# Trunk of two layers on one core: row multiplications on GpSimd, row scalings tied to chunks, operands emitted earlier

## The chip, the cores and the metric

The kernel runs on one core of a Trainium2 chip. A core has five engines with queues of their own: TensorE (PE, matmuls; PEld are its weight loads), VectorE (DVE), ScalarE (ACT), GpSimd (POOL) and SyncE (SP, which here only issues transfers). The metric is the device time of one execution in microseconds, the median of the runs shown.

## The reference

A sequence of 1024 rows and 1024 columns goes through two layers. Each layer is a mixer and a convolutional feed-forward network (FFN), and both end in a residual sum, a layer norm and a gain.

```python
e = jax.nn.silu(c @ cond_w + cond_b)
for i in range(DEPTH):
    mod = (e @ ada_w[i] + ada_b[i])[:, None, :]
    sh1, sc1, g1, sh2, sc2, g2 = jnp.split(mod, 6, axis=-1)
    y = mixers[i % N_MIXERS](x * (1.0 + sc1) + sh1)
    x = layer_norm(DN_ALPHA * x + (1.0 + g1) * y, ln_g[i, 0], ln_b[i, 0])
    y = conv_ffn(x * (1.0 + sc2) + sh2, ffn_up[i], ffn_conv_w[i], ffn_conv_b[i], ffn_down[i])
    x = layer_norm(DN_ALPHA * x + (1.0 + g2) * y, ln_g[i, 1], ln_b[i, 1])
```

The mixer of layer 0 is a gated delta net, that of layer 1 is retention: four heads, chunks of 128 rows, a state carried from chunk to chunk, each row of a head's output standardized and multiplied by a gate, then an output projection. Everything is float32.

## The kernel before

**Products.** Each float32 operand is split in two: ScalarE copies it into the high part (line 89) and VectorE subtracts that from the operand to make the low part (line 90). A product is then three matmuls: high by low, low by high, high by high (lines 110 to 112, 301 to 303, 716, 1585). Large products use schemes with seven block products in place of eight: `strassen` computes the input projections (the FFN's up and gate, retention's q, k and gate), and `proj_gen` the three projections back to 1024 columns, which are layer 0's FFN down, retention's output and layer 1's FFN down.

**The order.** The program emits instructions one after the other and gives them to a planner, which puts them in order on each engine by its own estimates, so an instruction can run well ahead of its place in the program. In the stretches with `pq`, `pm` and `ptr`, TensorE's order is written by hand: `run` walks several streams on a clock of its own (the dictionary `RL` has its delays). A load waits on SP until its buffer is free, and what is queued behind it on SP waits as well.

**The projections.** `proj_gen` runs seven block products. In each it loops over blocks `j`: `ops` loads and splits the pair of operands, twelve matmuls use it, and the next weight block is loaded (`load_b`, line 1451). When a product's sums are complete, `f1` to `f7` take them out. `finish` turns a sum of 128 x 512 into a residual row: it multiplies by the gate row G (line 1506), adds the scaled old row (line 1508) and takes statistics (line 1509). `norm` then needs a power, which runs on GpSimd (line 1516). `finish` runs 16 times in each projection, four times for each pair (half, nh). The pair (1, 0) gets its sum straight from PSUM, the other three from SBUF.

**Retention.** `ret_v` computes the values, half a head at a time, in four steps of two row blocks; its stream fills TensorE. `core` runs head by head through eight chunks, `ret_front` makes scores, `ret_back` finishes a chunk: statistics (line 1947), a power on GpSimd (line 1951), the normalized rows `on` (line 1953), their transposes on TensorE (line 719), the gate (loaded in line 1957, multiplied in line 1962), and the stores. Chunks 4 to 7 also load two blocks stored by chunk n - 4 (line 1980) and form four sums of blocks on GpSimd (line 1984). At the end of the last value product `ret_fill` starts the output projection, whose blocks fill TensorE beside head 3.

**Background work.** `bg` is a list of small units, one taken at each `bg_step`. For retention, `bg_gain` (lines 405 to 413) puts 16 units there, each of which loads 128 x 512 of the normalized rows, multiplies and adds the layer norm's gain and shift on GpSimd and stores the result `xg` for the residual of the output projection. `bg_ada` puts 8 units there that make the row G on VectorE (line 239). Their buffers have the tag "lane" (four, one held by the decay mask, two by the state) and "xT".

Of the kernel before, what the change touches and what calls it, by code (L numbers as in the profile page):

```python
# [12 lines left out]
ALU = mybir.AluOpType  # L13
# [20 lines left out]
def trunk_kernel(ctx: ExitStack, tc, A):  # L34
# [59 lines left out]
    def after(key):  # L94
        return tc.issue_after(anchor[key].ins) if key in anchor else nullcontext()
# [1177 lines left out]
    def c_of(q, a, b):  # L1273
# [2 lines left out]
        dve.tensor_tensor(b, a, b, ALU.add)  # L1276
        return b

    def strassen(hT0, xts, scale, shift, items, tags=("hTb", "hTb", "qkv", "qkv", "aux"), direct=False, late=()):
        B = {"11": hT0[:4], "21": hT0[4:]}  # L1280
        nblk = [0]
# [7 lines left out]
        def side(n, s):  # L1289
            out = []  # L1290
            for u in items[n][:2]:
                w = held.pop(u.offset, None) or load_w(u)
                if n == 0 and s == 0:
                    held[u.offset] = w
                X = acc_tile()
                for i, b in enumerate((("11", "21"), ("12", "22"))[s]):
                    for k in range(4):
                        mm3(X, w, k + 4 * i, B[b][k], i == 0 and k == 0, i == 1 and k == 3)
                out.append(X)
            return out  # L1300
# [121 lines left out]
    def proj_gen(nj, ablk, wsrc, slots, xsrc, G, final, ln_next, tag, ltags, dst, key, mm=pe.matmul, gate=None):  # L1422
# [80 lines left out]
            return x[nh] if isinstance(x, tuple) else x[:, hs(nh)]  # L1503

        def finish(half, t, nh, c):
            dve.tensor_tensor(c, c, G[nh], ALU.mult)
            xv = xh(half, t, nh)
            dve.scalar_tensor_tensor(xv, xv, ALPHA, c, ALU.mult, ALU.add)
            dve.bn_stats(stats[half][t][:, nh], xv)
# [82 lines left out]
        for st in steps[:ahead]:  # L1592
            load_b(*st)
        hooks = []
        for p, (an, bn, fin, side, fresh) in enumerate(prods):
            if gate and p < 2 or banks[side] is None:
                banks[side] = acc4() if gate and p < 2 or side == 0 else [sc_tile(), sc_tile(), mm_tile(), mm_tile()]
                if gate and p == 1:
                    banks[0] = banks[1]
                    banks[1] = None  # L1600
            accs = banks[0] if gate and p == 1 else banks[side]
            tail = []
            depth = ltags[3] if p == 6 else 2
            for j in range(nj):
                if gate and p < 2:
                    yield gate(j)
                    yield from take("qkv", 2)
                    give("qkv", 2)
                a, w = ops(an, bn, j, not gate and p < (7 if final else 5))
                with after("a"):  # L1610
                    for st in steps[p * nj + j + ahead:p * nj + j + ahead + 1]:
                        load_b(*st)
                if not gate and p == 2 and j % 2 == 0 and j < 8:
                    xload(0, j // 2)
                if final and p == 3 and j % 2 == 0 and j < 8:
                    xload(1, j // 2)
                if p == 2 and j < 4 and gate:
                    xload(0, j)
                    finish(0, j, 0, c11[j])
                if j >= nj - depth:  # L1620
                    tail.append((j, a, w))
                else:
                    for t in range(4):
                        mma(accs[t], t, a, w, fresh and j == 0, False, mm if p < 2 else pe.matmul if fresh else mm_on)
                        yield 0.0
                for _ in range(-(-20 // (nj - 1)) if p == 6 else 4 if p == 5 else 2):
                    if later:
                        later.pop(0)()
                if p == 5 and j > 1 and not later:
                    for _ in range(-(-16 // (nj - 2))):  # L1630
                        if hooks:
                            hooks.pop(0)()
                bg_step()
            while later:
                later.pop(0)()
            if p == 5:
                while hooks:
                    hooks.pop(0)()
            if p == 6:
                pin[0] = None  # L1640
            for t in range(4):
                for j, a, w in tail:
                    mma(accs[t], t, a, w, fresh and j == 0, j == nj - 1, mm if p < 2 else pm_on if p == 6 else pe.matmul if fresh else mm_on)
                fin(t, accs[t])
                yield 0.0
            if p == 1:
                yield "P2"
            if p == 4:
                hooks = [] if final else ln_hooks(0, xts[0], tag, ln_next, outs, dst, key, bal["h"])
                if not final:  # L1650
                    hooks += [lambda t=t: xload(1, t) for t in range(4)]
# [12 lines left out]
    def layer_tail(i, mix, wout, xsrc, x_mid, x_out, ln_next, final):  # L1664
        sc2, sh2 = fold(i, 1, 2 * i)
        if i == 0:
            bg_tag[0] = "xT"
            hT0 = []
            get = out_hl(mix)
            G1 = rows[0, 2]  # L1670
            xts = proj_ln(0, GH, get, wout, xsrc, G1, ("x", i), then=[lambda: bg_ada(0, 5, "row")])
            hooks = ln_hooks(0, xts, "hTa", lambda: (sc2, sh2), hT0, x_mid, ("mid", i), BAL["gh"])
            xts = proj_ln(1, GH, get, wout, xsrc, G1, ("x", i), hooks=hooks)
            hooks = ln_hooks(1, xts, "hTa", lambda: (sc2, sh2), [], x_mid, ("mid", i))
            for h in hooks[KT:]:
                h()
            bg_tag[0] = "wr"
        else:
            mix.append((sc2, sh2))
            hT0, xts = proj_st(mix[0])  # L1680
        bg_gain(2 * i, x_mid, xg[i + 1], "xT")
        if i == 0:
# [78 lines left out]
        while rowq or rowp:  # L1761
            row_step()
        slots = {"c": "hTa", "x": "qkv"}
        gb2 = gain_rows(3, ("mid", i), "hTb") if final else None
        return proj_st(proj_gen(NF // 2, ablk_of(ad, "qkv"), A["ffn_down"][i], slots, xg[i + 1], rows[i, 5],
                       (gb2, x_out) if final else None, ln_next, "hTb", ("hTb", "hTa", 8, 6, "f") if final else ("qkv", "hTa", 8, 4, "0"), x_out, ("out", i)))
# [91 lines left out]
    def ret_v(h, half):  # L1858
        accs = acc4()
        for kp in range(4):  # L1860
            wh, wl = load_w(A["ret_wv"][h, kp])
            for kk in range(2):
                kt = kp * 2 + kk
                hl = hT[half][kt]
                ns = slice(kk * 4, kk * 4 + 4)
                for t in range(4):
                    ts_ = slice(t * P, (t + 1) * P)
                    pm(accs[t], hl[1][:, ts_], wh[:, ns], start=(kt == 0), stop=False)
                    pm(accs[t], hl[0][:, ts_], wl[:, ns], start=False, stop=False)
                    pm(accs[t], hl[0][:, ts_], wh[:, ns], start=False, stop=(kt == KT - 1))  # L1870
                    yield 0.0
            bg_step()
        for t in range(4):
            yield from take("qkv", 2)
            vv = two("qkv", F32R, "vv")
            split(vv[0], vv[1], accs[t])
            va[h].append(vv)
        emit(("rv", h, half), RL["v"])
# [21 lines left out]

    def core(h):
        yield after_ev(("rv", h, 0), ("core", h - 1))
        if h == 2:
            bg_ada(1, 2, "row")
        q, k = load_qk(h, 0), load_qk(h, 1)
        St = None
        yield RL["q"]
        r = ret_front(h, 0, q, k)
# [36 lines left out]
    def ret_back(h, n, po):  # L1945
# [3 lines left out]
        dve.bn_aggr(mv[:, 0:2], st[:, 0])  # L1949
        dve.tensor_scalar(mv[:, 2:3], mv[:, 1:2], 1e-6, None, ALU.add)  # L1950
        pool.tensor_tensor(mv[:, 3:4], mv[:, 2:3], mhalf[:, 0:1], ALU.pow)
        on = tl("t2", [P, HALF], name="on")
        dve.tensor_scalar(on, po, mv[:, 0:1], mv[:, 3:4], ALU.subtract, ALU.mult)
        yield RL["b"]
        sl = slice(n * P, (n + 1) * P)
        g = tl("cv", [P, 516], name="gt")[:, 0:HALF]
# [3 lines left out]
            ptr(pt[:, j * P:(j + 1) * P], on[:, j * P:(j + 1) * P])  # L1960
        ot = tl("cv", [P, 516], name="ot")[:, 0:HALF]
        dve.tensor_mul(ot, pt, g)
        s4 = slice(n % 4 * P, (n % 4 + 1) * P)

        def pair_view(t):
            return t.rearrange("p (j a f) -> p a j f", a=2, f=P)

        def blk(nm):
            return od[2 * h:2 * h + 2, ABLK.index(nm), :, s4].rearrange("j p t -> p j t")

        ov = pair_view(ot)
        if n < 4:
            for a, nm in enumerate(("11", "12")):
# [1 line left out]
            if n == 3:  # L1975
                emit(("ob", h), RL["o"])
            return
        pv = pair_view(tl("cv", [P, 516], name="op")[:, 0:HALF])
        for a, nm in enumerate(("11", "12")):
            sp.dma_start(pv[:, a], blk(nm))  # L1980
        act.dma_start(blk("22"), ov[:, 1])
        for d, x, y, op, nm in ((ov[:, 0], ov[:, 0], ov[:, 1], ALU.add, "S1"), (pv[:, 0], ov[:, 0], pv[:, 0], ALU.subtract, "S2"),
                                (pv[:, 1], pv[:, 1], pv[:, 0], ALU.subtract, "S4"), (ov[:, 1], ov[:, 1], pv[:, 0], ALU.subtract, "S3")):
# [15 lines left out]
    def ret_fill():  # L1999
# [2 lines left out]
                yield from ret_v(h, half)  # L2002
        while bg or pend:
            bg_step()
        slots = {"c": "hTb", "x": "hTb"}
        mix.append(proj_gen(8, ablk_of(od, "qkv"), A["ret_wout"], slots, xg[0], rows[1, 2], None,
                            lambda: mix[1], "hTa", ("qkv", "hTb", 4, 4, "r"), xs[2], ("mid", 1), pm, lambda j: after_ev(("ob", j // 2))))
        for r in mix[0]:
            if r == "P2":
                return  # L2010
            yield r

    mix = []
    bg_gain(1, xs[1], xg[0])
    events["core", -1] = clk[0]
    free["qkv"] = 20
    bg_tag[0] = "xT"
# [105 lines left out]
```

## Time and profile before

| what | value |
|---|---|
| three runs | 2900.12, 2903.78 and 2907.11 us |
| median | 2903.78 us |
| profiled execution | 2897.41 us |
| its span, first to last instruction | 2895.6 us |
| mean granted TensorE clock | 0.989 |
| VectorE busy | 75% of the span |
| GpSimd busy | 17% of the span |

The profile is one execution. Its tables give busy time by engine, the granted clock of TensorE as a share of full speed, and, for a group of instructions or in order of time, what ended the idle time before them. An engine's busy time is the union of its instructions, so a matmul of 390 ns that starts every 226 ns counts 226. Retention with its output projection lies between 1720 and 2240 us, layer 1's FFN follows up to the end, and layer 0's down projection ends at 1391 us.

### The profile page before, as it was taken

How to read it: one execution, taken by the hardware profiler on the slowest of the kernel's cores; microseconds unless marked ns; L12 is line 12 of the kernel's file. 1: busy time of each engine (PE TensorE's matmuls, PEld its weight loads, DVE VectorE, ACT ScalarE, POOL GpSimd, SP SyncE). 2: the span in 40 equal slices, each digit the busy share in tenths (PEclk: the TensorE clock that was granted, in tenths of full speed). 3: DMA queues.
4: the chain of work that ended last, by engine and by line, in shares of the span. 5: the costliest groups of instructions: out<-in, count | busy, mean ns of one | idle time of the engine just before them, and what ended most of it. 6: DMA issues, size and time to landing. Idle time of an engine off the chain costs nothing.

```text
span 2895.6 us, 38913 instructions
## 1 busy us (share of the span) xinstructions
PE 2794.7 (97%) x13594; PEld 2284.7 (79%) x13594; DVE 2184.7 (75%) x3874; ACT 1295.0 (45%) x2387; POOL 490.4 (17%) x509
## 2 busy tenths in 40 slices
PE   8999999999999999999999999999999999999997
PEld 6777887887787878887888877777677788888886
DVE  5787688576788888868677656666689887777779
ACT  4663465344654444545333332222344644444443
POOL 0311221010023232000000022422201023332001
PEclk9998999999999999999999999999999999999999
DMA  7223243164254555845343365655664264434853
GB/s 277 88 95 121 85 139 103 52 240 153 95 189 163 195 181 171 294 153 189 127 146 127 119 233 159 211 165 156 214 217 146 71 196 138 142 132 163 287 182 117
DMA packets 252884, 465.30 MB, mean 161 GB/s; under 512 B 24144, under 2 KB 77776, under 8 KB 252688
## 3 DMA queue, kind: packets, MB, share of 16 engines
q1 hardware_dynamic: 218560, 408.02, 42.9%
q10 hardware_dynamic: 31488, 46.15, 4.3%
q0 software_dynamic: 2640, 8.65, 0.8%
q8 instruction: 107, 1.75, 0.3%
q14 instruction: 89, 0.73, 0.1%
HBM read 346.86 MB, written 115.87 MB: 160 GB/s over the span
## 4 chain that ended last, share of the span: by engine, by line
PE 54%; DVE 23%; DMA 10%; issue 6%; ACT 5%; POOL 1%; SPq 0%; ACTq 0%; DVEq 0%; POOLq 0%
PE acc L716 9%; PE acc L1285 5%; PE acc L1585 4%; PE acc L110 4%; PE acc L111 4%; PE acc L112 4%; PE sc L716 3%; PE sc L1285 3%; DVE o L1719 3%; PE mm L716 2%; DMA mvw<-in_ada_w 2%; DVE wb L90 2%; DMA wr<-in_ffn_up 2%; DVE qkv L490 2%; DVE mm L1339 2%
## 5 line engine op out<-in xcount | busy, mean ns | idle before, releaser
L716 PE MATMUL acc<-hT,wh 128*128 128x512 f32 x960 | 300.0, 394 | 0.0
L1585 PE MATMUL acc<-bb,ab 128*128 128x512 f32 x984 | 230.9, 393 | 6.9 <-DVE ab L90 3.3
L89 ACT ACTIVATE ab<-ar 128x512 fp32r<-128x512 f32 x210 | 131.1, 629 | 220.9 <-PE mm L303 48.3
L1585 PEld LDWEIGHTS acc<-bb,ab 128*128 128x128 f32 x984 | 184.1, 189 | 48.8 <-DVE ab L90 4.1
L716 PEld LDWEIGHTS acc<-hT,wh 128*128 128x128 f32 x960 | 182.8, 190 | 36.0
L90 DVE TENSOR_TENSOR ab<-ar,ab 128x512 fp32r<-128x512 f32 x210 | 149.0, 715 | 81.4 <-ACT ab L89 81.3
L1285 PE MATMUL acc<-T,wb 128*128 128x512 f32 x840 | 202.1, 389 | 0.4 <-DVE wb L90 0.4
L716 PE MATMUL acc<-hT,wl 128*128 128x512 f32 x480 | 197.2, 411 | 3.6 <-ACT sq L509 2.4
L89 ACT ACTIVATE wb<-mm 128x512 fp32r<-128x512 f32 x216 | 124.1, 597 | 167.3 <-DVE mm L1339 158.8
L411 POOL TENSOR_TENSOR xg<-xg,gb 128x512 f32<-128x512 f32 x48 | 66.2, 1380 | 709.5 <-DMA xg<-xs 405.6
L90 DVE TENSOR_TENSOR wl<-wr,wh 128x1024 fp32r<-128x1024 f32 x98 | 123.3, 1258 | 82.8 <-ACT wh L89 82.5
L1285 PEld LDWEIGHTS acc<-T,wb 128*128 128x128 f32 x840 | 157.5, 188 | 34.2 <-ACT o L1720 1.2
L89 ACT ACTIVATE wh<-wr 128x1024 fp32r<-128x1024 f32 x98 | 103.6, 1060 | 148.3 <-PE acc L716 60.1
L90 DVE TENSOR_TENSOR wb<-wr,wb 128x512 fp32r<-128x512 f32 x162 | 114.1, 705 | 64.1 <-ACT wb L89 64.0
L1750 POOL TENSOR_TENSOR o<-o 128x512 f32<-128x512 f32 x80 | 112.5, 1414 | 269.0 <-ACT pc L1355 175.2
L1719 DVE SCALAR_TENSOR_TENSOR o<-g,vc,o 128x512 f32<-128x512 f32 (+2 forms) x176 | 151.3, 870 | 8.1 <-ACT o L1714 6.9
L90 DVE TENSOR_TENSOR wb<-mm,wb 128x512 fp32r<-128x512 f32 x216 | 145.2, 686 | 6.9 <-ACT wb L89 6.9
L1339 DVE TENSOR_TENSOR mm<-wr 128x512 f32<-128x512 f32 x108 | 87.8, 813 | 76.7 <-DMA wr<-in_ffn_up 61.3
L89 ACT ACTIVATE wb<-wr 128x512 fp32r<-128x512 f32 x162 | 101.3, 626 | 94.0 <-PE acc L1285 28.4
L716 PE MATMUL acc<-wh,hT 128*128 128x512 f32 x384 | 135.5, 417 | 1.5 <-DVE vv L90 1.4
L1355 ACT ACTIVATE pc<-acc 128x512 f32<-128x512 f32 x143 | 84.3, 589 | 113.2 <-PE acc L1285 65.0
L239 DVE SCALAR_TENSOR_TENSOR ada<-mvw,e,ada 128x512 f32<-128x512 f32 x140 | 106.9, 763 | 23.7 <-DMA mvw<-in_ada_w 23.4
(672 smaller groups left out, 7420.0 us busy)
## 6 DMA issues: line engine op xcount, KB each, us to landing
wr<-in_ffn_up SPq DMA_DIRECT2D x92, 512.0 KB, 3.9
mvw<-in_ada_w SPq DMA_DIRECT2D x80, 512.0 KB, 4.4
ad<-o SPq DMA_DIRECT2D x154, 256.0 KB, 2.3
ar<-ad SPq DMA_DIRECT2D x154, 256.0 KB, 3.8
Br<-in_ffn_down SPq DMA_DIRECT2D x88, 256.0 KB, 3.5
wr<-in_ret_wv SPq DMA_DIRECT2D x32, 512.0 KB, 4.0
ar<-od SPq DMA_DIRECT2D x56, 256.0 KB, 5.2
wr<-in_gdn_wqkv SPq DMA_DIRECT2D x24, 512.0 KB, 3.6
```

Source lines behind the costliest of these rows:

```text
L89: anchor["sp"] = act.activation(dst_h, src, AF.Copy)
L90: eng.tensor_tensor(dst_l, src, dst_h, ALU.subtract)
L110: mm(acc, wl[:, k], hl[0], start=first, stop=False)
L111: mm(acc, wh[:, k], hl[1], start=False, stop=False)
L112: mm(acc, wh[:, k], hl[0], start=False, stop=last)
L239: dve.scalar_tensor_tensor(a, wr[:, kk], e[:, k:k + 1], a, ALU.mult, ALU.add)
L716: pq(pe.matmul(out, lhsT, rhs, start=start, stop=stop), cost or COST[out.shape[-1]])
L1285: return pe.matmul(*a, skip_group_check=True, **kw)
L1339: dve.tensor_tensor(t, x, y, op)
L1585: return pe.matmul(*args, skip_group_check=True, **kw)
L1719: dve.scalar_tensor_tensor(tv, gv[:, c0 - j:c1 - j], w[:, 2 - j:3 - j], tv, ALU.mult, ALU.add)
L1750: (dve if fp == 0 else pool).tensor_tensor(o[d], o[x], o[y], op)
```

## The change

There are four parts.

1. In `finish` the multiplication by G runs on GpSimd for all but the pair (1, 0).
2. The 16 gain units of retention leave the background list. `ret_back` now calls one `gain_step` right after the power of chunks 0 to 3 of each head, and of chunk 4 of the last head: it finishes the row loaded by the call before and loads the next one. With that list shorter, `ret_v` takes a background step at every other step in heads 0 to 2, and the units of G start at head 1 in place of head 2.
3. The output projection's first pair of operands is loaded and split before the matmuls of the last step of the last value product (`start_out`, which waits until head 3's q and k loads are emitted). In chunks 4 to 7 the two block loads move ahead of the gate load.
4. A projection that is followed by `strassen` loads and splits the first weight of that stage before its last sums (`preload`).

```diff
+    wpre, wnext_up = {}, []
+
+    def preload():
+        while wnext_up:
+            u = wnext_up.pop(0)
+            wpre[u.offset] = load_w(u)
...
-                w = held.pop(u.offset, None) or load_w(u)
+                w = held.pop(u.offset, None) or wpre.pop(u.offset, None) or load_w(u)
...
         def finish(half, t, nh, c):
-            dve.tensor_tensor(c, c, G[nh], ALU.mult)
+            (pool if True and (half, nh) != (1, 0) else dve).tensor_tensor(c, c, G[nh], ALU.mult)
...
+        ready = {}
+        if gate:
+            ready[0, 0] = ops(*prods[0][:2], 0, False)
+            with after("a"):
+                load_b(*steps[ahead])
+            yield "ops"
...
-                a, w = ops(an, bn, j, not gate and p < (7 if final else 5))
-                with after("a"):
-                    for st in steps[p * nj + j + ahead:p * nj + j + ahead + 1]:
-                        load_b(*st)
+                if (p, j) in ready:
+                    a, w = ready.pop((p, j))
+                else:
+                    a, w = ops(an, bn, j, not gate and p < (7 if final else 5))
+                    with after("a"):
+                        for st in steps[p * nj + j + ahead:p * nj + j + ahead + 1]:
+                            load_b(*st)
...
             if p == 6:
                 pin[0] = None
+                preload()
...
             mix.append((sc2, sh2))
+            wnext_up.append(A["ffn_up"][i][1])
...
+        if not final:
+            wnext_up.append(A["ret_wg"][2])
...
             wh, wl = load_w(A["ret_wv"][h, kp])
+            if (h, half, kp) == (RH - 1, 1, 3):
+                yield after_ev(("qk", h))
+                start_out()
...
-            bg_step()
+            if kp % 2 or h == RH - 1:
+                bg_step()
...
-        if h == 2:
+        if h == 1:
             bg_ada(1, 2, "row")
         q, k = load_qk(h, 0), load_qk(h, 1)
+        emit(("qk", h))
...
         pool.tensor_tensor(mv[:, 3:4], mv[:, 2:3], mhalf[:, 0:1], ALU.pow)
+        if n < 4 or h == RH - 1 and n == 4:
+            gains.pop(0)()
         on = tl("t2", [P, HALF], name="on")
         dve.tensor_scalar(on, po, mv[:, 0:1], mv[:, 3:4], ALU.subtract, ALU.mult)
...
+        if n > 3:
+            pv = pair_view(tl("cv", [P, 516], name="op")[:, 0:HALF])
+            for a, nm in enumerate(("11", "12")):
+                sp.dma_start(pv[:, a], blk(nm))
         yield RL["b"]
...
-        pv = pair_view(tl("cv", [P, 516], name="op")[:, 0:HALF])
-        for a, nm in enumerate(("11", "12")):
-            sp.dma_start(pv[:, a], blk(nm))
         act.dma_start(blk("22"), ov[:, 1])
...
-        slots = {"c": "hTb", "x": "hTb"}
-        mix.append(proj_gen(8, ablk_of(od, "qkv"), A["ret_wout"], slots, xg[0], rows[1, 2], None,
-                            lambda: mix[1], "hTa", ("qkv", "hTb", 4, 4, "r"), xs[2], ("mid", 1), pm, lambda j: after_ev(("ob", j // 2))))
         for r in mix[0]:
...
+    def start_out():
+        slots = {"c": "hTb", "x": "hTb"}
+        mix.append(proj_gen(8, ablk_of(od, "qkv"), A["ret_wout"], slots, xg[0], rows[1, 2], None,
+                            lambda: mix[1], "hTa", ("qkv", "hTb", 4, 4, "r"), xs[2], ("mid", 1), pm, lambda j: after_ev(("ob", j // 2))))
+        assert next(mix[0]) == "ops"
...
-    bg_gain(1, xs[1], xg[0])
+    gains, gx = [], []
+
+    def gain_step(m):
+        if gx:
+            x, c, rs, gb = gx.pop()
+            pool.tensor_tensor(x, x, gb[0], ALU.mult)
+            pool.tensor_tensor(x, x, gb[1], ALU.add)
+            sp.dma_start(xg[0][rs, hs(c)], x)
+        if m < 2 * NCH:
+            c, r = divmod(m, NCH)
+            if r == 0:
+                gbs.append([tl("auh", [P, HALF], name="gb") for _ in range(2)])
+                for t, nm in zip(gbs[-1], ("ln_g", "ln_b")):
+                    sp.dma_start(t, A[nm][1:2, hs(c)].to_broadcast([P, HALF]))
+            rs = slice(r * P, r * P + P)
+            x = tl("lane", [P, HALF], name="xg")
+            sp.dma_start(x, xs[1][rs, hs(c)])
+            gx.append((x, c, rs, gbs[-1]))
+
+    gbs = []
+    gains += [lambda m=m: gain_step(m) for m in range(2 * NCH + 1)]
```

More of the change, by code (lines that the diff above doesn't have):

```diff
@@ L1951, in ret_back, with pair_view, blk @@
         pool.tensor_tensor(mv[:, 3:4], mv[:, 2:3], mhalf[:, 0:1], ALU.pow)
+        if n < 4 or h == RH - 1 and n == 4:
+            gains.pop(0)()
         on = tl("t2", [P, HALF], name="on")
         dve.tensor_scalar(on, po, mv[:, 0:1], mv[:, 3:4], ALU.subtract, ALU.mult)
+        s4 = slice(n % 4 * P, (n % 4 + 1) * P)
+        def pair_view(t):
+            return t.rearrange("p (j a f) -> p a j f", a=2, f=P)
+        def blk(nm):
+            return od[2 * h:2 * h + 2, ABLK.index(nm), :, s4].rearrange("j p t -> p j t")
+        if n > 3:
+            pv = pair_view(tl("cv", [P, 516], name="op")[:, 0:HALF])
+            for a, nm in enumerate(("11", "12")):
+                sp.dma_start(pv[:, a], blk(nm))
         yield RL["b"]
@@ L1962, in ret_back @@
         dve.tensor_mul(ot, pt, g)
[L1963 to L1969, printed above, removed]
         ov = pair_view(ot)
```

## The prediction

> **What bounds the kernel now.** I read the page's busy times first, then the busy time in stretches of 20 us, then the engines in order of time around each stretch in which TensorE is not full.
>
> ```profile
> span 2895.6 us, 38913 instructions
> PE 2794.7 (97%) x13594; PEld 2284.7 (79%) x13594; DVE 2184.7 (75%) x3874; ACT 1295.0 (45%) x2387; POOL 490.4 (17%) x509
> ```
>
> TensorE is busy 97% of the span, so 2895.6 - 2794.7 = 101 us of idle TensorE, and what a lowered clock costs, are all that a rearrangement can win anywhere. The change leaves the matmuls alone. It can only shorten waits, and only in the second half, where its places are.
>
> ```profile
> 1320.00:1340.00 20.00, 17.53 (x73) 14.05 (x72) 19.09 (x41) 9.02 (x15) 4.17 (x4) 0.91 0.44 138
> 1360.00:1380.00 20.00, 17.93 (x85) 14.35 (x84) 19.06 (x31) 12.04 (x20) 0.59 (x1) 1.00 0.41 135
> 1720.00:1740.00 20.00, 20.00 (x90) 16.36 (x89) 4.68 (x6) 7.32 (x11) 0.00 (x0) 0.93 0.57 198
> 1820.00:1840.00 20.00, 16.77 (x72) 13.13 (x71) 9.66 (x14) 4.88 (x7) 14.73 (x15) 0.91 0.86 251
> 1900.00:1920.00 20.00, 19.53 (x88) 14.77 (x87) 11.09 (x17) 5.46 (x7) 10.32 (x13) 1.00 0.72 211
> 2180.00:2200.00 20.00, 18.64 (x77) 13.79 (x77) 20.00 (x40) 12.91 (x23) 2.47 (x3) 1.00 0.27 87
> 2200.00:2220.00 20.00, 18.86 (x89) 15.05 (x89) 20.00 (x32) 6.34 (x10) 2.26 (x3) 1.00 0.52 186
> 2860.00:2880.00 20.00, 18.40 (x80) 14.54 (x79) 20.00 (x39) 1.34 (x2) 0.85 (x1) 1.00 0.17 66
> ```
>
> After the stretch and its length come the busy time and count of PE, PEld, DVE, ACT and POOL, then the granted clock. There are two kinds of hole. In the late products of the three projections (1320 to 1380, 2180 to 2220, 2860 to 2880) VectorE is full and TensorE loses 1.1 to 2.5 us a stretch. In retention's first head (1820 to 1840) VectorE is half idle, GpSimd is at 14.73 of 20, and TensorE loses 3.23 us and runs at 0.91.
>
> **Part 1: row scalings behind the powers.** Here is the hole at 1828 in order of time (start, duration, engine, line, operation; in brackets the idle time and its releaser):
>
> ```profile
> 1822.50 0.15 DVE L1950 TENSOR_SCALAR mv<-mv 128x1 f32<-128x1 f32 x1
> 1823.36 1.30 POOL L411 TENSOR_TENSOR xg<-xg,gb 128x512 f32<-128x512 f32 x1 [0.78 <-DMA xg<-xs]
> 1824.73 1.26 POOL L412 TENSOR_TENSOR xg<-xg,gb 128x512 f32<-128x512 f32 x1
> 1825.96 0.72 POOL L1984 TENSOR_TENSOR ot<-ot 128x256 f32<-128x256 f32 x1
> 1826.64 0.55 POOL L1951 TENSOR_TENSOR mv<-mv,mhalf 128x1 f32<-128x1 f32 x1
> 1828.18 0.64 PE L719 MATMUL mm<-cst,on 128*128 128x128 f32 x4 [3.23 <-DVE on L1953]
> ```
>
> The power's input was ready at 1822.65. It started at 1826.64, behind one scaled row (two operations) and a block sum; then VectorE normalized, and TensorE's transposes, whose place in its order is fixed, waited 3.23 us. The same step in head 1, where no scaled row is near:
>
> ```profile
> 1907.32 0.15 DVE L1950 TENSOR_SCALAR mv<-mv 128x1 f32<-128x1 f32 x1
> 1907.97 0.55 POOL L1951 TENSOR_TENSOR mv<-mv,mhalf 128x1 f32<-128x1 f32 x1
> ```
>
> starts 0.50 us after its input. The change puts every scaled row behind the power of one of chunks 0 to 3 (and the last behind head 3's chunk 4); those chunks have no block sums. What should go is 3.23 us of idle and 20 x (1 - 0.91) = 1.8 us of clock, less the 20 - 19.53 = 0.47 us that head 1 still loses in the like stretch: 4.6 us. Bounds: 0, if the power still stands behind something, and 5.0.
>
> The moved work is 16 rows, each with one load, two Pool operations and one store, and four loads of gain and shift rows. Pool's two operations take 2.56 us. Between two powers of early chunks it has room for them:
>
> ```profile
> 1874.32 0.55 POOL L1951 TENSOR_TENSOR mv<-mv,mhalf 128x1 f32<-128x1 f32 x1 [8.45 <-DVE mv L1950]
> ```
>
> 8.45 us idle hide 2.56; without that cover each row would cost up to 2.56 us of the next power. On SP the rows' 36 transfers now stand among the gate and weight loads of all four heads. Today some of them stand somewhere worse, at the end of the stage before:
>
> ```profile
> 1705.97 3.98 SPq L413 DMA_DIRECT2D xg<-xg  x2
> ...
> 1712.41 0.98 SPq L1854 DMA_DIRECT2D xlo<-xs  x2
> ...
> 1718.23 0.44 PE L282 MATMUL mm<-cst,xlo 128*128 128x128 f32 x2 [2.01 <-DMA xlo<-xs]
> ```
>
> SP stood 3.98 us on stores that wait for Pool, with the loads of the lower rows queued behind them, and TensorE waited 2.01 us for those loads. Tied to the chunks, the rows can no longer be drawn forward to this place. I take 2.0 us. Bounds: 0, as these loads also need a free buffer, and 2.0 plus the clock's 20 x (1 - 0.93) = 1.4 us just after, 3.4. The ada rows move from head 2 to head 1 (8 loads, 16 VectorE operations), and half of the background steps go. No TensorE wait of size stands there: 0.
>
> **Part 2: operands split ahead.** The output projection starts with
>
> ```profile
> 2028.71 0.40 PE L716 MATMUL acc<-wh,22_12806 128*128 128x512 f32 x1
> 2029.64 0.62 ACT L89 ACTIVATE ab<-ar 128x512 fp32r<-128x512 f32 x1
> 2031.10 0.68 DVE L90 TENSOR_TENSOR ab<-ar,ab 128x512 fp32r<-128x512 f32 x1
> 2031.84 3.02 PE L716 MATMUL acc<-bb,ab 128*128 128x512 f32 x12 [2.73 <-DVE ab L90]
> ```
>
> TensorE has no filler and waits 2.73 us for the first pair's splits. The change emits this pair (one load and two splits for each of its two operands) before the last quarter of the last value product, so the split is done when that ends. The first pair feeds 12 matmuls, 2.7 us, in which the second pair's splits fit (0.6 us each on ScalarE and VectorE). I take 2.7 us. Bounds: 0, if the wait passes to the second pair, and 2.7. The value product now also waits until head 3's q and k loads are issued; head 3 is in its second chunk by then, so this costs 0. The block loads drawn ahead of the gate load in chunks 4 to 7 help block sums that are not what TensorE waits for after part 1, but they take a buffer earlier: 0, with 2.7 either way, the size of the wait just quoted.
>
> **Part 3: first weights split ahead.**
>
> ```profile
> 1375.43 1.23 DVE L90 TENSOR_TENSOR wl<-wr,wh 128x1024 fp32r<-128x1024 f32 x1
> ...
> 1391.52 0.39 PE L110 MATMUL acc<-hT,wl 128*128 128x512 f32 x1
> ```
>
> ```profile
> 2213.33 1.23 DVE L90 TENSOR_TENSOR wl<-wr,wh 128x1024 fp32r<-128x1024 f32 x1
> ...
> 2223.53 0.48 PE L110 MATMUL acc<-hT,wl 128*128 128x512 f32 x1
> ```
>
> Both first weights are already split 15 and 9 us before their first matmul. Emitting load, copy and split earlier moves nothing that is late: 0. The most it could cost is one split, 1.2 us, ahead of the last sums.
>
> **Part 4: rows multiplied on GpSimd.** Twelve of 16 in each projection move, 36 in all.
>
> ```profile
> 2210.32 2.50 DVE L1506 TENSOR_TENSOR pa<-pa,rowb 128x512 f32<-128x512 f32 x4
> 2212.73 0.70 DVE L1508 SCALAR_TENSOR_TENSOR xt<-xt,pa 128x512 f32<-128x512 f32 x1
> ```
>
> Four take 2.41 us to the next start: 0.60 us of VectorE each. On Pool the same shape takes 1.30 us:
>
> ```profile
> L411 POOL TENSOR_TENSOR xg<-xg,gb x48: 1263/1295/1757, 835.0 to 2628.6; 128x512 f32<-128x512 f32 x48
> L1516 POOL TENSOR_TENSOR mv<-mv,mhalf x24: 548/926/3406, 1331.1 to 2888.7; 128x1 f32<-128x1 f32 x24
> ```
>
> and here the two engines meet:
>
> ```profile
> 1827.51 1.27 POOL L411 TENSOR_TENSOR xg<-xg,gb 128x512 f32<-128x512 f32 x1 [0.32 <-DMA op<-od]
> 1827.95 1.91 DVE L90 TENSOR_TENSOR wl<-wr,wh 128x1024 fp32r<-128x1024 f32 x1
> ```
>
> A split of 1.23 us took 1.91 beside a Pool multiplication, 0.68 lost; and the tiny power, 0.55 us alone, takes up to 3.4 us in the projections. So a row on Pool saves 0.60 us of VectorE and gives some back. Only rows where VectorE is full count: in layer 0's down projection four at 1318 to 1328 and four at 1361 to 1366, in retention's the eight from 2175 to 2212, in the last one the eight from 2818 to 2863: 24. Bounds for each: +0.60 saved, if nothing is given back, and 1.30 - 0.60 = 0.70 lost, if VectorE stands for the whole Pool operation. The measured meeting gives 0.60 - 0.68 = -0.08; I take 0. The stall it adds: VectorE's fused step (L1508) now waits for Pool, and behind it on VectorE are the splits of the next pairs, which TensorE waits for.
>
> The Trainium skill (SBUF — State Buffer, section "Who interferes with whom") says that a VectorE instruction with two SBUF inputs contends with a GpSimd one that reads SBUF, and that the shared port is held for the whole instruction, the other side standing fully still. By that rule nearly all splits and sums here contend and part 4 is a loss; the 1.91 us row agrees with it, one row deciding little about an average.
>
> **The sum.** -4.6 - 2.0 - 2.7 + 0 + 0 = -9.3 us, so a span of 2886.3. The profiled run took 2897.4 us in all, 1.8 above its span; the three runs without profile have a median of 2903.8, to which I apply the same difference: 2894.5.
>
> **The rivals.** A: the port decides. In the three full stretches each moved row costs VectorE 0.70 us net, 24 x 0.70 = 16.8; with -9.3 that is +7.5, so 2911. It is slower from 9.3 / 24 = 0.39 us a row on. For it: the two meeting rows; against: VectorE's statistics and sums out of PSUM, which lie between, may fill the time that Pool holds the port. The rule of the Trainium skill (SBUF — State Buffer, "Who interferes with whom") would make this of the time. B: nothing is given back. The gain in the full stretches is at most what TensorE loses there, 2.47 + 2.07 + 1.36 + 1.14 + 1.60 = 8.6 us and 1.8 us of clock at 1320: -9.3 - 10.4 = -19.7, so 2884. For it: Pool has nothing else to do there; against: the powers' 3.4 us. C: the change doesn't do what it says; the power stays late behind block sums, or the scaled rows' SP transfers hold gate loads up, and part 1's 4.6 us remain: -4.7, so 2899. For it: block sums stand ahead of the power in the rows above too; against: head 1.
>
> **How the numbers follow.** The forecast has 0.42, A 0.27, B 0.15, C 0.16. About 0.2%, 5.8 us, is what a measurement of this kernel tells from no change: its three runs spread 7 us. Faster: forecast and B, and a little of C, 0.58; slower: A, 0.27; within: 0.15. The range goes from B's 2885 to A's 2911; the forecast's own is 2888 to 2899.
>
> **What would show it.** Right: no wait of transposes near 3 us in retention's first head and a clock of 1.00 there; scaled rows directly behind powers; the wait of 2.73 us at the output projection's first matmul gone; no wait for the lower rows' load. Wrong: VectorE operations in the projections far above 0.69 us beside Pool multiplications of 1.3 to 3 us, and TensorE idle in the late products above the 8.6 us of now. If head 1 to 3 show new waits of transposes, the rows' transfers or the earlier buffers are at fault.

## The result, and the profile after

| | before | after |
|---|---|---|
| median of 12 runs each, one chip | 2905.99 us (2898.55 to 2912.63) | 2911.12 us (2907.65 to 2917.02) |
| ratio after/before | | 1.0015, 95% interval 1.0004 to 1.0026 |
| profiled execution | 2897.41 us, span 2895.6 | 2910.14 us, span 2908.2 |

The change makes the kernel slower by 0.15%, 4.4 us (by the ratio; the medians differ by 5.1), where 9.3 us less was forecast. From here on the parts have the prediction's numbers: part 1 is the row scalings, part 2 the early operands, part 3 the early weights, part 4 the multiplications on GpSimd (2, 3, 4 and 1 in the list of the change). The page of after begins:

```profile
span 2908.2 us, 38946 instructions
## 1 busy us (share of the span) xinstructions
PE 2800.0 (96%) x13594; PEld 2290.6 (79%) x13594; DVE 2185.3 (75%) x3838; ACT 1294.9 (45%) x2387; POOL 550.0 (19%) x545
```

VectorE lost 36 instructions of 0.69 us, 24.8 us of work (21.6 at the 0.60 us from one start to the next), and its busy time went from 2184.7 to 2185.3. So its other instructions became about as much longer.

The stretches of 20 us of after, in the columns of before:

```profile
1320.00:1340.00 20.00, 15.48 (x62) 12.32 (x61) 17.10 (x32) 5.96 (x10) 7.71 (x6) 0.91 0.39 132
1360.00:1380.00 20.00, 16.59 (x73) 12.94 (x72) 18.82 (x27) 14.04 (x26) 9.17 (x5) 0.91 0.37 119
1720.00:1740.00 20.00, 20.00 (x98) 16.44 (x96) 6.08 (x7) 7.31 (x11) 0.00 (x0) 1.00 0.65 226
1820.00:1840.00 20.00, 19.59 (x89) 15.13 (x88) 10.88 (x17) 5.67 (x8) 9.66 (x11) 1.00 0.71 213
1900.00:1920.00 20.00, 19.59 (x89) 15.13 (x88) 11.27 (x17) 5.85 (x8) 8.81 (x11) 1.00 0.82 239
...
2180.00:2200.00 20.00, 16.78 (x72) 12.76 (x70) 20.00 (x38) 12.28 (x23) 4.57 (x4) 1.00 0.31 98
2200.00:2220.00 20.00, 18.78 (x91) 15.35 (x90) 18.81 (x26) 10.10 (x17) 12.33 (x6) 1.00 0.41 157
2860.00:2880.00 20.00, 14.23 (x56) 10.26 (x54) 18.82 (x28) 3.65 (x6) 13.40 (x4) 0.87 0.14 53
```

In retention (1720, 1820) the clock is at 1.00, and of the 3.23 us that TensorE lost at 1820, 0.41 are left: part 1 worked there. In the five stretches of the projections TensorE's idle time went from 8.6 to 4.52 + 3.41 + 3.22 + 1.22 + 5.77 = 18.1 us, and the clock fell to 0.91 at 1360 and 0.87 at 2860. The moved rows, grouped by the line that multiplies them (nanoseconds: least, median, most):

```profile
L1513 POOL TENSOR_TENSOR pa<-pa,rowb x20: 1255/1694/8827, 1321.1 to 2874.0; 128x512 f32<-128x512 f32 x20
...
L1513 POOL TENSOR_TENSOR u<-u,rowb x12: 1288/1734/1753, 1292.0 to 2795.7; 128x512 f32<-128x512 f32 x12
L1513 DVE TENSOR_TENSOR acc<-acc,rowb x12: 674/700/700, 1391.0 to 2895.6; 128x512 f32<-128x512 f32 x12
```

One took 8.8 us. Here it is, in order of time (LDWEIGHTS rows left out):

```profile
2862.32 13.40 POOL L1513 TENSOR_TENSOR pa<-pa,rowb 128x512 f32<-128x512 f32 x4 [6.74 <-DVE pa L1572]
2862.70 0.69 DVE L1535 TENSOR_TENSOR xt<-xt,rowb 128x512 f32<-128x512 f32 x1
2863.30 0.69 DVE L1572 TENSOR_TENSOR pa<-u,pa 128x512 f32<-128x512 f32 x1
2863.90 0.69 DVE L90 TENSOR_TENSOR bb<-Br,bb 128x512 fp32r<-128x512 f32 x1
...
2868.72 0.69 DVE L1536 TENSOR_TENSOR xt<-xt,rowb 128x512 f32<-128x512 f32 x1
...
2869.32 0.69 DVE L90 TENSOR_TENSOR ab<-ar,ab 128x512 fp32r<-128x512 f32 x1
...
2871.18 1.74 DVE L1515 SCALAR_TENSOR_TENSOR xt<-xt,pa 128x512 f32<-128x512 f32 x1 [1.18 <-POOL pa L1513]
2872.84 1.75 DVE L90 TENSOR_TENSOR ab<-ar,ab 128x512 fp32r<-128x512 f32 x1
2874.51 1.76 DVE L1515 SCALAR_TENSOR_TENSOR xt<-xt,pa 128x512 f32<-128x512 f32 x1
2874.64 1.49 PE L1592 MATMUL acc<-bb,ab 128*128 128x512 f32 x3 [3.61 <-DVE ab L90]
...
2876.93 1.65 PE L1592 MATMUL acc<-bb,ab 128*128 128x512 f32 x3 [0.80 <-DVE ab L90]
...
2879.94 1.65 PE L1592 MATMUL acc<-bb,ab 128*128 128x512 f32 x3 [1.36 <-DVE ab L90]
```

While VectorE issues one instruction with two SBUF inputs behind the other, GpSimd's multiplication, ready at 2862, gets nowhere. At 2870 VectorE comes to the step that needs the product and has to stop; now GpSimd runs, and each VectorE instruction that starts beside one of its next three multiplications takes 1.74 to 1.76 us in place of 0.69. TensorE's pair stands behind them: 3.61 us, then 0.80 and 1.36.

The meetings can be counted. Of the 128x512 VectorE instructions that the timeline of the three projections shows singly and that overlap a moved multiplication, 47 have two inputs in SBUF: 27 of them took 1.09 to 1.78 us, the other 20 their usual 0.67 to 0.70. Another 14 have at most one input in SBUF (statistics, sums out of PSUM): all took 0.68 or 0.69.

The span differs by more (12.6 us) than the medians, and a table of stretches says where. Each is measured between the same TensorE instructions of all kernels (first and last matmul of each projection, first of retention; the output projection's row starts with the first product that comes after retention, at 2106.5 before):

| us | before | after | parts 1 to 3 | part 4 alone |
|---|---|---|---|---|
| start to layer 0's down projection | 1170.7 | 1173.4 | 1184.3 | 1175.9 |
| that projection | 221.0 | 225.8 | 219.2 | 226.0 |
| up to retention | 324.1 | 323.3 | 321.9 | 326.4 |
| retention | 390.7 | 383.9 | 384.0 | 389.7 |
| rest of its output projection | 116.4 | 119.6 | 116.2 | 120.3 |
| up to the last projection | 446.3 | 446.3 | 450.0 | 448.3 |
| last projection to the end | 226.3 | 235.9 | 225.6 | 234.1 |

The first row has none of the edits in it and differs by 13.6 us between executions, so whole spans are not compared below. The other rows hold to about 3 us: one kernel that was profiled twice (part 1 alone) had 387.2 and 383.9 in retention. After gained 6.8 us in retention, and lost 4.8 + 3.2 + 9.6 = 17.6 in the projections. In these three rows TensorE's idle time rose from 9.3 to 21.8 us, and what the lowered clock takes (each stretch times what its granted clock lacks of 1) from 7.8 to 13.3: 18.0 more in all, so longer waits and a lower clock account for the loss.

### The profile page after: what moved, and what is told of

Its sections match the earlier page's. It is cut to its first block, busy times and chain, and to the rows that moved or that the text cites. A ratio compares the mean times of both kernels' runs of the same rounds, so it can differ in the third digit from the quotient of the medians.

```text
span 2908.2 us, 38946 instructions
## 1 busy us (share of the span) xinstructions
PE 2800.0 (96%) x13594; PEld 2290.6 (79%) x13594; DVE 2185.3 (75%) x3838; ACT 1294.9 (45%) x2387; POOL 550.0 (19%) x545
## 4 chain that ended last, share of the span: by engine, by line
PE 55%; DVE 22%; DMA 11%; ACT 6%; issue 5%; POOL 1%; SPq 0%; ACTq 0%; DVEq 0%; POOLq 0%
PE acc L716 8%; PE acc L1292 5%; PE acc L1592 4%; PE acc L110 4%; PE sc L716 4%; PE acc L111 4%; PE acc L112 4%; PE sc L1292 3%; DMA mvw<-in_ada_w 3%; PE mm L716 3%; DVE wb L90 2%; DVE o L1737 2%; DVE qkv L490 2%; DVE ada L239 2%; DVE mm L1346 1%
## 5 line engine op out<-in xcount | busy, mean ns | idle before, releaser
L1592 PE MATMUL acc<-bb,ab 128*128 128x512 f32 x984 | 237.5, 400 | 20.2 <-DVE ab L90 11.5
L411 POOL TENSOR_TENSOR xg<-xg,gb 128x512 f32<-128x512 f32 x32 | 45.4, 1418 | 397.4 <-DMA xg<-xs 397.4
```

The costliest lines, as they stand in the source:

```text
L1592: return pe.matmul(*args, skip_group_check=True, **kw)
```

## The experiments

All against the kernel before on the same chip, five rounds. The difference is the ratio's, of 2907 us.

| run | median us | ratio, 95% interval | us |
|---|---|---|---|
| parts 1 to 3 | 2895.59 | 0.9965, 0.9950 to 0.9981 | -10.2 |
| part 4 alone | 2924.63 | 1.0063, 1.0043 to 1.0083 | +18.3 |
| parts 1 to 3, idle multiplications, unplaced | 2906.45 | 0.9997, 0.9985 to 1.0009 | -0.9 |
| parts 1 to 3, 32 of 512 columns on GpSimd | 2897.60 | 0.9968, 0.9954 to 0.9981 | -9.3 |
| parts 1 to 3, idle multiplications, placed | 2920.73 | 1.0037, 1.0024 to 1.0051 | +10.8 |
| parts 1 to 3, memsets, placed | 2898.36 | 0.9967, 0.9952 to 0.9981 | -9.6 |
| parts 1 to 3, rows u and c on GpSimd | 2896.92 | 0.9955, 0.9940 to 0.9970 | -13.1 |
| parts 1 to 3, rows pa on GpSimd | 2913.84 | 1.0020, 1.0008 to 1.0032 | +5.8 |
| part 1 alone | 2904.97 | 0.9992, 0.9983 to 1.0002 | -2.3 |
| part 1 alone, again | 2905.70 | 0.9991, 0.9976 to 1.0005 | -2.6 |
| part 2 alone | 2905.73 | 0.9993, 0.9979 to 1.0006 | -2.0 |
| parts 1 and 2 | 2895.60 | 0.9962, 0.9948 to 0.9976 | -11.0 |

### Which part loses

The first run undoes part 4, the second does nothing else.

```
-            (pool if True and (half, nh) != (1, 0) else dve).tensor_tensor(c, c, G[nh], ALU.mult)
+            dve.tensor_tensor(c, c, G[nh], ALU.mult)
```

> Changed kernel with the 36 multiplications back on VectorE: the row scalings, the early operands and the early first weights are left. Theory (the 36 multiplications on GpSimd are the whole loss): 6 to 10 us faster than the kernel before (ratio 0.9966 to 0.998), the late products of the three projections as before (TensorE idle 3.7, 3.5 to 4.7 and 1.6 us in them). Rival (the loss in the projections comes from the other three parts, by another order of instructions there): no faster than before, and TensorE's waits of 4.5 and 3.6 us in the late products stay.

> Kernel before with only the 36 multiplications on GpSimd. Theory: 10 to 20 us slower than before (ratio 1.0035 to 1.007): 7.5, 3.3 and 9.0 us were lost in the three projections of the changed kernel's profile, and one execution may overstate it. Rival: within 3 us of before.

Both came as the theory has them (the first 0.2 us beyond its range): -10.2 and +18.3, which add up to +8.1 beside the 4.4 of the whole change, within the sum of their intervals. Part 4 alone lengthens the same three rows of the table as the whole change does, and shows the same 3.6 us wait in the last projection. Without part 4 that wait is gone:

```profile
2871.43 1.66 PE L1592 MATMUL acc<-bb,ab 128*128 128x512 f32 x6 [0.44 <-DVE ab L90]
2873.84 13.22 PE L1592 MATMUL acc<-bb,ab 128*128 128x512 f32 x57 [0.74 <-DVE ab L90]
```

Taken from the whole change and from parts 1 to 3, part 4 costs (1.0015 - 0.9965) x 2907 = 14.5 us, some 5 either way by the two intervals.

### What of GpSimd's work costs

Two things come with a moved row: GpSimd's instruction beside VectorE's, and VectorE's wait for the product. In the next runs VectorE multiplies all rows itself, so nothing waits for GpSimd.

```
...
             dve.tensor_tensor(c, c, G[nh], ALU.mult)
+            if (half, nh) != (1, 0):
+                pool.tensor_tensor(dum, G[nh], G[nh], ALU.mult)
```

> As the run of parts 1 to 3, multiplications on VectorE, and beside each of the 36 GpSimd multiplies two constant rows into a row that nobody reads, so that GpSimd's 128x512 instruction is there and nobody waits for its result (its result is left unused). Theory (a GpSimd multiplication and VectorE's instructions shut each other out, so it costs VectorE its own length whoever needs the result): 8 to 25 us slower than the run of parts 1 to 3, with VectorE instructions of 1.2 to 1.8 us beside the GpSimd ones. Rival (the loss is VectorE's queue standing behind the wait for GpSimd's result): within 3 us of the run of parts 1 to 3.

This run missed its place. Nothing in it ties GpSimd's instructions to the rows, and they ran long before, the first at 704.9:

```profile
L1516 POOL TENSOR_TENSOR dum<-rowb x36: 1034/1290/1902, 704.9 to 2438.8; 128x512 f32<-128x512 f32 x36
```

It lost 9.3 us against parts 1 to 3, and VectorE's busy time rose by 12.4 us, but in other places: in its profile the two FFN projections take 219.9 and 226.1 us, as in parts 1 to 3. That 9.3 lies in the theory's range is luck; for the question it says nothing. The next one reads the row just multiplied (`dum, c, G[nh]`), which holds it at its place:

> The idle multiplications of the earlier run, now held at their place: each reads the row that VectorE has just multiplied, and writes a row that nobody reads (so its result is left unused). VectorE keeps all 48 multiplications and waits for GpSimd nowhere. Theory (GpSimd's 128x512 multiplication and VectorE's instructions with two SBUF inputs shut each other out): 10 to 25 us slower than the run of parts 1 to 3, 2906 to 2921 us, with VectorE's busy time up by some 25 us (36 times 0.7). Rival (only VectorE's wait for a product costs): within 4 us of the run of parts 1 to 3.

It is 20.9 us slower than parts 1 to 3, and VectorE's busy time rose from 2184.1 to 2206.0 us with the same 3874 instructions. So the wait isn't needed for the loss. (In part 4 VectorE is also spared the 36 multiplications, so its 14.5 us need not be the same.) Is it that GpSimd is busy, or what it reads? The next edit, against the placed multiplications:

```
-                pool.tensor_tensor(dum, c, G[nh], ALU.mult)
+                pool.tensor_tensor(dum[:, 0:1], c[:, 0:1], G[nh][:, 0:1], ALU.mult)
+                pool.memset(dum, 0.0)
+                pool.memset(dum, 1.0)
```

> As the idle multiplications held at their place, with each replaced by a product of one column (it reads SBUF for a moment, and holds the place) and two memsets of 128x512, which read nothing: GpSimd is as busy as there, 1.1 to 1.6 us for each of the 36 rows, and VectorE waits for it nowhere (the memsets' result is left unused). Theory (the two engines shut each other out where both read SBUF): within 5 us of the run of parts 1 to 3, ratio 0.996 to 0.998, VectorE's busy time up by less than 8 us. Rival (any GpSimd work beside VectorE costs): as slow as the held multiplications, 12 us or more above the run of parts 1 to 3, ratio 1.001 or more.

The first line of busy times is that of the placed multiplications, the second that of the memsets:

```profile
PE 2810.1 (96%) x13594; PEld 2296.6 (79%) x13594; DVE 2206.0 (76%) x3874; ACT 1296.3 (44%) x2387; POOL 572.1 (20%) x545
```

```profile
PE 2800.6 (97%) x13594; PEld 2290.5 (79%) x13594; DVE 2181.0 (75%) x3874; ACT 1296.9 (45%) x2387; POOL 569.0 (20%) x617
```

GpSimd is as busy in both, at the same places, but not with the same work: of the memset run's 80 us there 42 are the one-column products, some of which stood waiting for up to 8.94 us, and 38 are memsets. The memsets themselves met no hindrance and made none. All 72 have one length (nanoseconds: least, median, most):

```profile
L1517 POOL MEMSET dum<- x36: 524/527/532, 1299.7 to 2877.3; 128x512 f32 x36
L1518 POOL MEMSET dum<- x36: 524/527/531, 1300.3 to 2877.9; 128x512 f32 x36
```

Of the 56 VectorE instructions of 128x512 with two inputs in SBUF that overlap one, none took more than 0.74 us; beside the placed multiplications 28 of 77 took more than 1 us. Multiplications that read SBUF cost 20.9 us; memsets cost 0.6, inside the interval. This is the rule of the Trainium skill (SBUF — State Buffer, "Who interferes with whom"): a VectorE instruction with two SBUF inputs contends with a GpSimd one that reads SBUF, not with one that only writes, nor does a VectorE one with at most one SBUF input (outside the 2-port modes) contend. The counts agree: 27 in 47 and 0 in 14 in the kernel after, 0 in 56 beside memsets.

The opposite case keeps the hand-over and shortens the instruction: VectorE multiplies 480 columns, GpSimd 32.

> As the run of parts 1 to 3, but of each of the 36 rows VectorE multiplies 480 columns and GpSimd 32, so that each hand-over to GpSimd and back stays and its instruction is short. Theory (what counts is the length of GpSimd's instruction): within 4 us of the run of parts 1 to 3. Rival (the hand-over and VectorE's wait for it count): as slow as the changed kernel, 10 us or more above the run of parts 1 to 3.

0.9 us above parts 1 to 3: 36 hand-overs by themselves cost nothing that can be told. Its longest 128x32 product took as long as a whole row's, since VectorE's run of instructions kept it out too:

```profile
L1517 POOL TENSOR_TENSOR pa<-pa,rowb x20: 248/664/8520, 1335.5 to 2878.3; 128x32 f32<-128x32 f32 x20
```

### Which rows

> As the run of parts 1 to 3, with only the rows u (12) and c (4) multiplied on GpSimd: VectorE has short idle stretches around them. Theory (the exclusion costs where VectorE is full): 1 to 6 us above the run of parts 1 to 3. Rival (each moved row costs the same): 16 of 36 rows, 6 to 7 us above it.

> As the run of parts 1 to 3, with only the 20 rows pa (8 of the first half's first columns and 12 of the second half's last) multiplied on GpSimd, among VectorE's fullest stretches. Theory: 9 to 14 us above the run of parts 1 to 3. Rival (each moved row costs the same): 20 of 36 rows, 8 us above it. Together with the other run the two should make up the 14 to 15 us between the changed kernel and the run of parts 1 to 3.

The 16 rows u and c: 2.9 us under parts 1 to 3, no difference by the intervals, where 1 to 6 above was expected; VectorE's busy time fell by 6.8 us (2184.1 to 2177.3) of the 11 that left it. The 20 rows pa: 16.0 us above, 0.80 a row (some 0.3 either way), where 9 to 14 us was expected; VectorE's busy time rose by 1.9 us though 13.8 left it. Both misses lie within the intervals; one price for each row does not. Rows c show why (one line for GpSimd's four, then VectorE's):

```profile
2101.74 5.76 POOL L1513 TENSOR_TENSOR c<-c,rowb 128x512 f32<-128x512 f32 x4 [13.10 <-DVE c L1547]
2102.33 0.69 DVE L1547 TENSOR_TENSOR c<-acc,pa 128x512 f32<-128x512 f32 x1 [0.67 <-PE acc L716]
2103.69 0.69 DVE L1547 TENSOR_TENSOR c<-acc,pa 128x512 f32<-128x512 f32 x1 [0.67 <-PE acc L716]
2105.05 0.69 DVE L1547 TENSOR_TENSOR c<-acc,pa 128x512 f32<-128x512 f32 x1 [0.67 <-PE acc L716]
...
2106.28 1.77 DVE L1466 TENSOR_TENSOR Bw<-Br,Bw 128x512 f32<-128x512 f32 x1
```

The sums out of PSUM run beside GpSimd at full speed, with idle time between; of the two VectorE instructions there with both inputs in SBUF one took 0.70 us, and the other, the last row shown, 1.77.

Rows u are not spared the exclusion: in the run of u and c, 12 of the 13 VectorE instructions with two SBUF inputs that met a multiplication took 1.02 to 1.78 us. What spares the time is TensorE. From 2 us before the first row u to 12 us after the last, it is never idle in the two FFN projections, in this run as in before, though VectorE is full there too (12.00 of 12 us at 1288 in before). In the output projection it idles 2.93 us there in this run, and 1.2 to 2.3 in before and the runs that keep u on VectorE.

### Parts 1, 2 and 3

> Part 1 alone: the row scalings behind the powers (with the SyncE order and the background work's places that go with it); operands and first weights split as before, multiplications on VectorE. Prediction's own terms: 4.6 + 2.0 = 6.6 us faster than before, no wait of 3.23 us for a power in head 0 and none for the lower rows; the wait of 2.73 us before the first product of the output projection stays. Rival (the gain of parts 1 to 3 comes from the early operands and weights): within 3 us of before.

> Parts 1 and 2 without the first weights split ahead, multiplications on VectorE. Prediction's term for part 3 is 0, so this should be as fast as the run of parts 1 to 3: within 4 us of 2896, ratio 0.995 to 0.998, with TensorE's wait for the first weights' split at the output projection's end unchanged at 3 to 4 us. Rival (part 3 carries what part 1 alone did not bring, 8 us): ratio 0.998 to 1.000. Part 2 against part 1 alone: the 2.73 us wait gone, retention 3 us shorter.

Adding part 3 to parts 1 and 2 costs 0.9 us: nothing that can be told. But part 1 alone brought 2.3, where its terms had 6.6, and with part 2 11.0. So part 2 was run alone, with part 1 alone beside it:

> Part 2 alone: kernel before with the first operands of the output projection split ahead, and the ada rows in head 1, which this needs; row scalings as before. Prediction's own term: 2.7 us faster than before (ratio 0.9991), the wait of 2.73 us gone, retention 3 us shorter, and the waits of 2.01 and 3.23 us that part 1 removes still there. Rival (part 2 brings the 8 us that separate part 1 alone from parts 1 and 2): ratio 0.9965 to 0.998.

> Part 1 alone once more, beside part 2 alone on one chip. If the first time is right, 0 to 5 us faster than before (0.9983 to 1.0002), and short of the prediction's 6.6; the profile's stretches (the stage before retention 2 us shorter, retention 3.5 us) say 5.5 less 1.4 in the output projection, 4 us.

The runs of part 1 alone keep the block loads ahead of the gate load, that of part 2 alone leaves them where they were, and both parts' runs have the ada rows in head 1. Each alone brings 2 to 3 us with an interval that touches 0; together they bring 11.0 (7 to 15). Part 2 alone lost its 2.73 us wait, but its retention took 390.4 us in place of 390.7, not the 3 us less that were expected: it got a longer wait at the start:

```profile
1707.54 4.26 SPq L413 DMA_DIRECT2D xg<-xg  x2
...
1714.25 0.91 SPq L1863 DMA_DIRECT2D xlo<-xs  x2
1721.01 0.69 PE L282 MATMUL mm<-cst,xlo 128*128 128x128 f32 x2 [4.04 <-DMA xlo<-xs]
```

The stores of scaled rows are still ahead of the lower rows' load on SP, 4.26 us in place of 3.98; counted from retention's first matmul (1716.6, and 1715.8 before) the load is issued 1.1 us later, and TensorE's 2.01 us became 4.04. Why it came later (part 2 alone has the ada rows in head 1, and the row scalings still in the background) this trace doesn't show. Part 1 takes just this wait away (no run with part 1 has it), which would explain some 2 us. Each run alone also has a new wait of TensorE of 1.2 to 1.8 us beside the ada rows (between 1935 and 1960), so 2.3 + 2.0 pays for that twice. The rest of the excess of 11.0 over 2.3 + 2.0 stays open; by the intervals the whole excess is barely above noise.

## Why the prediction was wrong

**The step that failed** is part 4's "I take 0" for a row in a full stretch, between 0.60 us saved and 0.70 lost. It rested on one meeting (a split that took 1.91 in place of 1.23 us) and on the hope that statistics and sums out of PSUM would fill the time. Those do run free, but in the fullest stretches VectorE issues splits, differences and scalings, nearly all with two SBUF inputs. There a GpSimd multiplication and VectorE's instructions take turns, and GpSimd's turn is longer (1.3 us against 0.6). Measured: 14.5 us, or 0.60 for each of the 24 rows counted; 0.80 for each of the 20 rows pa. Rival A ("the port decides") had 0.70 a row, 16.8 us and 2911 us. Its mechanism is shown by the placed multiplications and the memsets. That the result is 2911.12 is in part luck: A had +7.5 us on a median of 2903.8, and +4.4 came on 2905.99. The choice of rows was right for the 20 rows pa; the other 4 of the 24, u in the output projection, are among the 16 that together cost nothing that can be told. "Where VectorE is full" was not the right test for it: VectorE is full around the rows u of the FFN projections too, and TensorE waits for none of it there. The low end of the range is a slip: B's own sum is 2884, not 2885.

**The wait the prediction feared** (VectorE's fused step behind GpSimd) exists, 3 times and 3.5 us in all. The one shown follows a multiplication that was kept out for 8.8 us; by itself the hand-over costs nothing that can be told (0.9 us for 36). How much of the 14.5 us these waits make was not measured apart.

**Parts 1 and 2** came as forecast in sum: 9.3 forecast, 10.2 and 11.0 measured with part 3 and without. The terms did not: part 1 alone, 6.6 forecast, measured 2.3 and 2.6, so the sum's agreement is partly luck. In the trace of after the waits of 2.01, 3.23 and 2.73 us, 7.97 together, are gone, and the clock in the stretches at 1720 and 1820 is 1.00 in place of 0.93 and 0.91, 3.2 us. Scaled rows run ahead of a chunk's power without delaying it, and the output projection's first matmuls have no wait in brackets:

```profile
1788.61 1.28 POOL L2050 TENSOR_TENSOR xg<-xg,gb 128x512 f32<-128x512 f32 x1 [4.94 <-DMA xg<-xs]
1789.97 1.34 POOL L2051 TENSOR_TENSOR xg<-xg,gb 128x512 f32<-128x512 f32 x1
1791.89 0.15 DVE L1975 TENSOR_SCALAR mv<-mv 128x1 f32<-128x1 f32 x1
1792.12 0.55 POOL L1976 TENSOR_TENSOR mv<-mv,mhalf 128x1 f32<-128x1 f32 x1 [0.81 <-DVE mv L1975]
...
2030.31 2.94 PE L716 MATMUL acc<-bb,ab 128*128 128x512 f32 x12
```

Of 7.97 + 3.2 = 11.2 us, 6.8 remained in retention. One new wait that the prediction had put at 0 is the ada rows':

```profile
1957.35 0.75 DVE L239 SCALAR_TENSOR_TENSOR ada<-mvw,e,ada 128x512 f32<-128x512 f32 x1 [1.52 <-DMA mvw<-in_ada_w]
1958.03 0.17 DVE L1974 BATCH_NORM_AGGREGATE mv<-rst 128x2 f32<-128x6 f32 x1
...
1960.48 0.96 PE L716 MATMUL sc<-vv,kz 128*128 128x512 f32 x3 [2.04 <-DVE on L1980]
```

VectorE stood 1.52 us for an ada weight, with the chunk's statistics queued behind, and TensorE waited 2.04. The wait at the last chunk grew from 2.61 to 3.72, and two of 0.98 and 0.68 are new. Here the step "no TensorE wait of size stands there: 0" priced the place the rows left, not the one they went to.

**Part 3**: 0 forecast, 0.9 slower measured. The wait for a weight's split after the output projection's end, 1.70 us before, is 3.44 after and 3.26 without part 3, so part 3 neither made it nor cured it. Part 4 alone has 3.44 too, part 1 alone 4.05 and 4.27, part 2 alone 3.31: no one part makes it, and its cause stays open.

**The sum**: -9.3 with part 4's 0 replaced by the measured 14.5 gives +5.2; measured +4.4. The version that beats both kernels is the change without the rows pa on GpSimd: parts 1 to 3 at 0.9965 or, with rows u and c on GpSimd, 0.9955, which the intervals don't tell apart.

## What to carry to other kernels

Before moving an elementwise instruction to GpSimd, look at what VectorE runs beside it. Where that was mostly instructions with two SBUF inputs back to back and TensorE stood behind them, a 1.3 us multiplication on GpSimd cost more here than the 0.6 us it took off VectorE, and its result came late as well; beside sums out of PSUM, statistics or idle time, or where TensorE waited for nothing, it cost nothing that could be told. To price an overlap, run the work once at its place with nobody waiting for it, and tie it there by a data dependence; without one, 36 multiplications ran far from their place here.

## What was not expected of the hardware

GpSimd can be kept out for long, whatever its instruction's size: 8.83 us for a multiplication of 128x512, 8.52 for one of 128x32 and 8.94 for one of 128x1 in the memset run, each beside an unbroken run of VectorE instructions in the last projection:

```profile
2865.46 8.94 POOL L1516 TENSOR_TENSOR dum<-pa,rowb 128x1 f32<-128x1 f32 x1 [0.25 <-DVE pa L1514]
...
2873.67 0.67 DVE L1541 TENSOR_TENSOR xt<-xt,rowb 128x512 f32<-128x512 f32 x1
2874.27 0.67 DVE L1521 BATCH_NORM_STATS2 st<-xt 128x6 f32<-128x512 f32 x1
```

GpSimd's instruction of 0.19 us ends at 2874.40, just after VectorE comes to statistics, which have one input in SBUF. In the kernel after, the long multiplication ended when VectorE had to wait for it.
